# Attention, second half: ScalarE's operations on rows fetched from DRAM kept in program order, the last output weights split one tile later each

## The chip, the cores and the metric

The kernel runs on one core of a Trainium2 chip. The metric is the time of one execution on the device, in microseconds (us). Five engines work side by side, each through its own queue and in the order of that queue: TensorE (PE, matrix products), VectorE (DVE), ScalarE (ACT), GpSimd (POOL) and SyncE (SP), which here issues nearly all DMA transfers.

## The reference

One encoder layer on x of 2048 tokens by 1024 columns, in float32. The tokens form a grid of 32 rows by 64 columns.

```
h    = layernorm(x) * (1 + scale) + shift            # shift, scale, gate from silu(c) @ ada_w + ada_b
proj = h @ w_in                                      # 1024 x 9216
q_h, i_h, zf, zb, g_h, q_n, k_n, v_n, g_n = split(proj)
y_hg = rmsnorm(scan_forward + scan_backward) * silu(g_h)     # 8 heads of 128, gated linear recurrence
o_na = softmax(q k^T / 8 + bias, over an 8 x 16 window) v    # 16 heads of 64, on the grid
y_na = o_na * silu(g_n)
out  = layernorm(2**0.25 * x + gate * (concat(y_hg, y_na) @ w_out)) * ln_g + ln_b
```

The change touches the neighbourhood attention (q_n, k_n, v_n, g_n) of the second half of the tokens, and the preparation of w_out.

## The kernel before

Every large product is done in three passes on pairs of reduced-precision parts: a float32 operand is split into a high part (ScalarE copies it, which rounds) and a low part (VectorE subtracts the high part from the raw one). TensorE multiplies high by high, high by low and low by high. So a block of weights costs a DMA, one ScalarE operation and one VectorE operation before TensorE can use it.

The program has four stages: the attention of the first half of the tokens; the recurrence (`hgrn`) of both halves; the attention of the second half; and the rest of the output projection with the last layer norm. The change lies in the third, which is some 600 us long.

There the work goes in eight **units** u = 0 to 7, one for each pair of heads. A unit has twelve **tiles**: three groups of query rows R = 1, 2, 3 by four column blocks j. For a tile, `scores` multiplies Q by the keys (L1000, L1003), VectorE adds the bias and takes the maximum (L1012), ScalarE takes the exponential (L1017), VectorE normalises (L1021, L1022), TensorE transposes (`turned`, L1044), VectorE and ScalarE copy the transposes out of PSUM (L1048, L1050), and `sums` multiplies by V (L1063). After tile 4 of a row group the result is multiplied by the gate (L1073) and stored. A tile is turned one step, and summed two steps, after its scores.

While a unit's tiles run, TensorE fills the gaps with the dense products of the next unit (`natten_stream`, L278: q, k and gate columns), or in unit 7 with the first four token blocks of the output projection (`out_stream`, L1428 to L1430). `weave` deals these out by a running share, two steps per tile. In unit 0 the stream begins with the last products for v (`vstream`, L291, copied out of PSUM at L297).

After each tile i, `natten_woven` calls what its lists name for **slot** i: `prep_now` (this unit's last pieces), `prep_next` (the next unit's pieces) and `extra`. The pieces are those of `Prep`: `q(R)` makes two split Q tiles (L926 to L929), `k(i)` writes a piece of the shared key tiles KA, KB, KL (L941, then a DMA that copies the piece within the tile, L942, and L943), `gate(R)` takes silu (an exponential at L956, then `sigmoid`, L337 to L339, with two more ScalarE operations, and L958), `v(c)` loads V (L950), and `table` loads the bias (L722 to L730). Row groups 2 and 3 take q, k and gate from products that this stage has just made. Row group 1 and the first two key pieces belong to tokens of the first half: their products were stored in DRAM long ago, and `fetch` brings them back into four buffers `bk` (L913). There are four such buffers for four rows per unit (q, k0, k1, g), so a fetch waits until an earlier row has been used.

In units 6 and 7, `extra` also holds the preparation of the output weights: `wo_load(n, blocks)` loads blocks of 128 rows by 512 columns (column half n) into six buffers (four of `vt`, two of `gt`, L1383), and `wo_split` splits them (L1388, L1389) into tiles that held the dense products' left operand (`hts`). `y_early` and `y_split` do the same for the left operand of the output projection (L1394, L1420, L1421).

**What sets the order.** TensorE's queue in this stage is written out by hand: it is the program order. The other queues are ordered by a planner, which runs a simulated timeline over the program and issues, on each engine, the operation that it takes to be ready, the earlier in program order first; a block under `high_priority` counts as 1500 places earlier. It can move an operation far ahead of its place if the simulated transfer has landed by then. `keep_in_program_order` (called `pinned` in the file, L127) takes one operation and puts it behind the operation that was traced last before it on the same engine. It adds no wait. It holds against that one neighbour only: if the neighbour can move, the pinned operation can move with it. Before the change, `wo_split`, `y_split` and the split of the dense weights (L778) are pinned; `q`, `k` and `gate` are not.

Of the kernel before, what the change touches and what calls it, by code (L numbers as in the profile page):

```python
# [13 lines left out]
AF = mybir.ActivationFunctionType  # L14
# [24 lines left out]
def body(ctx: ExitStack, tc: tile.TileContext, t):  # L39
    nc = tc.nc  # L40
    dve, act, pool, pe = nc.vector, nc.scalar, nc.gpsimd, nc.tensor
    dma = nc.sync.dma_start
    x, out = t["x"], t["out"]
# [9 lines left out]
    @contextmanager  # L53
    def psum_phase(name, psb, pmap={}):
        with tc.tile_pool(name="p" + name, bufs=1, space=PSUM, reuse_waits="tile") as q:
            cur.update(psum=q, ps=psb, map=pmap)
            yield

    @contextmanager
    def phase(name, bufs, smap={}):  # L60
        with tc.tile_pool(name=name, bufs=1, reuse_waits="tile") as p:
            cur.update(pool=p, bufs=bufs, smap=smap)
            yield
# [28 lines left out]
    def tl(tag, dt=F32, shape=None):  # L92
        if tag in cur["smap"]:
            tag = cur["smap"][tag]
            return sh.tile([P, 512], dt, tag=tag, name=nm(tag), bufs=SH[tag])
        return cur["pool"].tile([P, 512] if shape is None else shape, dt, tag=tag, name=nm(tag), bufs=cur["bufs"].get(tag, 1))
# [50 lines left out]
    def mod_load(k):  # L147
        mod["w", k] = tl("ada", shape=[P, 2 * D])
        dma(mod["w", k], t["ada_m"][k])
# [186 lines left out]
    def sigmoid(e):  # L336
        dve.tensor_scalar_min(e, e, ECAP)  # L337
        act.activation(e, e, AF.Ln, bias=1.0)
        act.activation(e, e, AF.Exp, scale=-1.0)  # L339
# [331 lines left out]
    def bias_fill():  # L671
        bigt = tl("big", shape=[P, 448])
        pool.memset(bigt, BIG)
        rows = tint.rearrange("a j q r h k -> (a j q) (r h k)").rearrange("(x y) m -> y x m", y=P)
        src = bigt.rearrange("p (o m) -> p o m", o=1).to_broadcast([P, 3, 448])
        pinned(dma(rows[:, :, 0:448], src))
        pinned(dma(rows[:, :, 960:1408], src))
# [57 lines left out]
    def natten_init(n, half):  # L735
        pbuf.clear()
        cur["bias"] = (11, 15)[half]
        for i in range(n):
            b = tl("pbuf")
            pool.memset(b[:, 352:512], 0.0)  # L740
            pbuf.append(b)
        keysets.clear()
        for i in range(2 - half):
            keysets.append({z: tl(f"{z}{i}", F32R, [P, (12, 28)[half] * GW]) for z in ("KA", "KB", "KL")})
# [116 lines left out]
    def natten_stream(p, half, feed=None, bygroup=False):  # L861

        raws = {n: [None, None] for n, _ in NCOL}

        def gen():
            for gs in ((0,), (1,)) if bygroup else ((0, 1),):
                for n, c in NCOL:
                    if feed:
                        i = feed.at
                        feed.at += 1  # L870
                        feed.split(i + 1)
                        feed.load(i + 2)
                        his, los = feed.tiles[i]
                    else:
                        wv = t["w_in"][(c + p * P) // P]
                        his, los = load_split(lambda i: wv[:, i * 512:(i + 1) * 512], 2)
                    for g in gs:
                        pz = ps("pj")
                        for k in range(KT):
                            proj_mm(pz, his, los, g, k)  # L880
                            if k == KT - 1:
                                raws[n][g] = evac(pz)
                            if feed and g == gs[-1] and k == 2:
                                feed.split(i + 2)
                            yield KUS
        return raws, gen()
# [4 lines left out]
    def vstream(*pairs):  # L891
        for p2 in pairs:
            for _ in vproj(t["w_v"][p2], nv_d[p2], 1):
                yield 2.9
# [8 lines left out]
    class Prep:  # L903
# [17 lines left out]
        def q(self, R):  # L921
            raw = self.src("q", R)
            rv = raw.rearrange("p (r j c) -> p j r c", j=4, c=16)[:, :, ::-1, :]
            a, b = tl("Q", F32R), tl("Q", F32R)
            av, bv = (z.rearrange("p (j r c) -> p j r c", j=4, c=16) for z in (a, b))
            act.activation(av[0:64], rv[0:64], AF.Copy)  # L926
            act.activation(bv[64:128], rv[64:128], AF.Copy)
            dve.tensor_tensor(av[64:128], rv[0:64], av[0:64], op=ALU.subtract)
            dve.tensor_tensor(bv[0:64], rv[64:128], bv[64:128], op=ALU.subtract)  # L929
            self.Q[R] = (a, b)  # L930

        def k(self, i):
            a, b, src, off = KPIECE[self.half][i]
            n = (b - a) * GW
            raw = (self.bk[src] if src in self.bk else self.raws["k"][src])[:, off:off + n]
            o = slice(a * GW, b * GW)
            top, bot = slice(0, 64), slice(64, 128)
            keys = keysets[self.p % len(keysets)]
            for z, x, y in (("KA", top, bot), ("KB", bot, top)):
                z = keys[z]  # L940
                act.activation(z[x, o], raw[x], AF.Copy)  # L941
                dma(z[y, o].bitcast(F32), z[x, o].bitcast(F32))  # L942
                dve.tensor_tensor(keys["KL"][x, o], raw[x], z[x, o], op=ALU.subtract)  # L943

# [8 lines left out]
        def gate(self, R):  # L953
            raw = self.src("g", R)
            sg = tl("sg")
            act.activation(sg, raw, AF.Exp, scale=-1.0)  # L956
            sigmoid(sg)
            dve.tensor_tensor(sg, raw, sg, op=ALU.mult)  # L958
            self.sg[R] = sg
# [156 lines left out]
    def turn(pipe, n):  # L1116
        if len(pipe) >= n:
            m, r, c, ss = pipe[-n]
            pipe[-n][3] = m.turned(r, ss)
# [295 lines left out]
    def y_split(*tts):  # L1415
        for tt in tts:
            for q in range(2):
                hi = wp.tile([P, 512], F32R, tag="whi", name=nm("yh"), bufs=4)
                lo = wp.tile([P, 512], F32R, tag="wlo", name=nm("yl"), bufs=4)
                tc.keep_in_program_order(act.activation(hi, yraws[tt, q], AF.Copy))  # L1420
                dve.tensor_tensor(lo, yraws[tt, q], hi, op=ALU.subtract)  # L1421
                yhl[tt, q] = hi, lo
# [70 lines left out]
    with psum_phase("n1", NPS), phase("n1", NB1, SM1), tc.manual_schedule(engines={mybir.EngineType.PE}):  # L1493
        natten_init(5, 1)
        st = st0
        for f, *a in ((st.k, 0), (st.k, 1), (st.k, 2), (st.q, 1), (st.table, "mid", 0), (st.table, "mid", 1), (st.v, 2), (st.v, 3), (st.table, "mid", 3), (st.q, 2), (st.v, 4), (st.gate, 1)):
            f(*a)
        vs = vstream(2, 3)
        for _ in range(5):
            next(vs)  # L1500
        pipe = []
        cts = [(c + u * P) // P for u in range(1, 8) for _ in range(2 if u == 7 else 1) for n, c in NCOL]
        feed = Feed(cts)
        feed.at = 0
        for u in range(8):
            nxt, extra = None, None
            if u < 7:
                raws, dense = natten_stream(u + 1, 1, feed, u + 1 == 7)
                total = NLEN
                if u == 0:  # L1510
                    dense, total = chain(vs, dense), NLEN + 1.375 * VLEN
                nxt = Prep(u + 1, 1, raws)
                if u == 6:
                    extra = {4: [(wo_load, 0, 0, 1)], 5: [(wo_load, 0, 2, 3, 4, 5)], 7: [(wo_split, 0, 0, 1)], 8: [(wo_split, 0, 2, 3), (wo_load, 0, 6, 7)],
                             9: [(wo_split, 0, 4, 5)], 10: [(wo_split, 0, 6, 7), (wo_load, 1, 0, 1, 4, 5), (y_early, 0)], 11: [(wo_load, 1, 2, 3), (y_early, 1)]}
            else:
                y_split(0, 1)
                dense, total = out_stream(list(range(NE))), NE * 16 * KUS
                extra = {0: [(wo_split, 1, 0, 1), (wo_load, 1, 6, 7)], 1: [(wo_split, 1, 2, 3)], 2: [(wo_split, 1, 4, 5, 6, 7)]}
            weave(natten_woven(st, nxt, pipe, extra), dense, total, 24)  # L1520
            st = nxt
        m, r, c, pts = pipe.pop(0)
        m.sums(r, c, pts)
        turn(pipe, 1)
        m, r, c, pts = pipe.pop(0)
        m.sums(r, c, pts)
# [72 lines left out]
```

## Time and profile before

| | us |
|---|---|
| three runs: median (lowest, highest) | 2688.76 (2688.58, 2693.19) |
| the profiled execution | 2689.12 |
| span of its profile | 2687.3 |
| TensorE busy in the span | 2607.6 (97%) |
| VectorE, ScalarE busy | 1766.4 (66%), 1421.6 (53%) |
| second half of the attention | about 1764 to 2374 |

The time of an execution holds the span of the profile and a little around it. In the rows below an instruction has its start, its duration, its engine, its line in the kernel, the tile that it writes and those that it reads, and in brackets how long its engine had been idle before it and what ended that. A busy share alone does not tell what a microsecond saved on an engine is worth; that is read from where TensorE waits, and for whom.

### The profile page before, as it was taken

The page shows a single profiled execution, that of the slowest core. Times are in us where ns is not written, and L with a number is a line of the kernel's source. Part 1 is how long each engine was busy: PE and PEld are TensorE (multiplying, and loading weights), DVE is VectorE, ACT ScalarE, POOL GpSimd, SP SyncE. Part 2 cuts the span into 40 slices and gives each one's busy share as a digit, 9 for nine tenths or more (in the row PEclk, how much of TensorE's full clock was granted, in tenths as well). Part 3 has the DMA queues.
Part 4 walks back from the last instruction along what each step waited for, and adds up shares of the span by engine and source line. Part 5 has one row for each costly group of instructions (what it writes and reads, how often), then busy time and mean ns, then how long its engine had stood idle before and what let it go on. Part 6 is the DMA issues. An engine that isn't in the chain of part 4 may idle for free.

```text
span 2687.3 us, 46049 instructions
## 1 busy us (share of the span) xinstructions
PE 2607.6 (97%) x17332; PEld 2153.6 (80%) x17332; DVE 1766.4 (66%) x4354; ACT 1421.6 (53%) x2808; POOL 105.8 (4%) x142
## 2 busy tenths in 40 slices
PE   6999999989999999999999999989999999899998
PEld 5888788878888888888888888877777777678887
DVE  7445545377777778778877787445777778548443
ACT  4533445366666666666666666445666666431110
POOL 0000000000000000000000000000000000032221
PEclk8999999999999999999999999999999999999999
DMA  7476454212111136212222222344444445344331
GB/s 270 138 210 146 139 174 143 87 49 72 64 60 60 64 94 212 72 44 71 75 71 79 66 71 91 106 141 127 128 127 128 128 131 142 101 146 133 98 94 55
DMA packets 225550, 295.94 MB, mean 110 GB/s; under 512 B 28599, under 2 KB 117431, under 8 KB 224183
## 3 DMA queue, kind: packets, MB, share of 16 engines
q1 hardware_dynamic: 225327, 293.00, 36.0%
q8 instruction: 136, 2.23, 0.4%
q14 instruction: 87, 0.71, 0.1%
HBM read 217.72 MB, written 66.99 MB: 106 GB/s over the span
## 4 chain that ended last, share of the span: by engine, by line
PE 72%; DVE 2%; DMA 2%; ACT 1%; issue 1%; SPq 0%; DVEq 0%; ACTq 0%
PE pj L278 39%; PE ps L1428 4%; PE ps L1430 4%; PE ps L1429 4%; PE ps L1063 3%; PE ps L1044 3%; PE pj L291 2%; PE ps L478 2%; PE ps L1000 1%; PE ps L470 1%; PE ps L1003 1%; PE ps L545 1%; PE ps L569 1%; PE ps L517 1%; PE ps L571 1%; PE ps L643 1%
## 5 line engine op out<-in xcount | busy, mean ns | idle before, releaser
L278 PE MATMUL pj<-h,wh 128*128 128x512 f32 x4000 | 1277.0, 400 | 4.5 <-ACT wh L803 2.1
L278 PEld LDWEIGHTS pj<-h,wh 128*128 128x128 f32 x4000 | 722.6, 188 | 162.5 <-issue 21.4
L278 PE MATMUL pj<-h,wl 128*128 128x512 f32 x2000 | 783.5, 392 | 0.0
L278 PEld LDWEIGHTS pj<-h,wl 128*128 128x128 f32 x2000 | 375.4, 188 | 83.1 <-DVE wl L804 0.4
L1017 ACT ACTIVATE pbuf<-pbuf,mx 128x480 f32<-128x480 f32 (+2 forms) x256 | 164.3, 643 | 182.3 <-DVE mx L1012 181.5
L1012 DVE CUSTOM_DVE_ANT_1 pbuf<-ps,bias 128x480 f32<-128x480 f32 (+2 forms) x256 | 144.1, 595 | 134.6 <-PE ps L1003 121.4
L291 PE MATMUL pj<-wh,h 128*128 128x256 f32 x1024 | 199.3, 289 | 10.2 <-ACT vt L297 9.9
L291 PEld LDWEIGHTS pj<-wh,h 128*128 128x128 f32 x1024 | 165.6, 194 | 14.9 <-ACT vt L297 10.8
L268 ACT ACTIVATE wh<-wr 128x512 fp32r<-128x512 f32 x192 | 120.2, 626 | 79.6 <-PE pj L278 69.1
L269 DVE TENSOR_TENSOR wl<-wr,wh 128x512 fp32r<-128x512 f32 x192 | 131.5, 685 | 42.9 <-ACT wh L268 41.4
L291 PE MATMUL pj<-wl,h 128*128 128x256 f32 x512 | 146.0, 285 | 0.0
L1050 ACT ACTIVATE pt<-ps 128x512 f32<-128x512 f32 (+1 forms) x128 | 69.0, 539 | 124.2 <-PE ps L1044 124.0
L1044 PE MATMUL ps<-ident,pbuf 128*128 128x128 f32 x896 | 119.4, 273 | 11.1 <-DVE pbuf L1022 11.1
L1048 DVE COPY pt<-ps 128x512 f32<-128x512 f32 (+1 forms) x128 | 79.3, 620 | 75.7 <-PE ps L1044 74.8
L1044 PEld LDWEIGHTS ps<-ident,pbuf 128*128 128x128 f32 x896 | 105.4, 141 | 27.2 <-issue 12.3
L464 DVE TENSOR_TENSOR de<-e,de 128x512 f32<-128x512 f32 x64 | 44.3, 692 | 118.7 <-ACT de L463 118.7
L1022 DVE TENSOR_SCALAR pbuf<-pbuf,mx 128x480 f32<-128x480 f32 (+2 forms) x256 | 107.9, 438 | 5.0
L1063 PE MATMUL ps<-pt,V 128*64 128x128 f32 x1376 | 104.3, 282 | 4.1 <-DVE pt L1048 3.4
L1404 ACT ACTIVATE yh<-yr 128x512 fp32r<-128x512 f32 x52 | 32.6, 628 | 129.3 <-PE ps L1429 107.2
L291 PEld LDWEIGHTS pj<-wl,h 128*128 128x128 f32 x512 | 99.3, 194 | 1.4 <-issue 0.5
L1477 DVE TENSOR_TENSOR vt<-ps,gt 128x512 f32<-128x512 f32 x24 | 16.5, 692 | 127.0 <-PE ps L1430 127.0
L1063 PEld LDWEIGHTS ps<-pt,V 128*64 128x64 f32 x1376 | 73.3, 136 | 31.1 <-issue 18.4
(268 smaller groups left out, 4646.9 us busy)
## 6 DMA issues: line engine op xcount, KB each, us to landing
wr<-in_w_in SPq DMA_DIRECT2D x276, 256.0 KB
yr<-yq SPq DMA_DIRECT2D x64, 256.0 KB
V<-nv SPq DMA_DIRECT2D x248, 64.0 KB
bias<-tint SPq DMA_DIRECT2D x24, 480.0 KB
x<-in_x SPq DMA_DIRECT2D x32, 256.0 KB
ada<-in_ada_m SPq DMA_DIRECT2D x8, 1024.0 KB
wr<-in_w_v SPq DMA_DIRECT2D x32, 256.0 KB
nv<-vt SPq DMA_DIRECT2D x32, 256.0 KB
```

Of the source, the lines that this page charges most:

```text
L268: act.activation(hi, raw, AF.Copy)
L269: dve.tensor_tensor(lo, raw, hi, op=ALU.subtract)
L278: pe.matmul(pz, a, b, start=(k == 0 and n == 0), stop=(k == KT - 1 and n == 2))
L291: pe.matmul(pzs[tp][:, i * 256:(i + 1) * 256], a, b, start=(k == 0 and n == 0 and i == 0), stop=(k == KT - 1 and n == 2), skip_group_check ...
L1012: return dve.tensor_tensor_reduce(s[:, 0:nk].rearrange("p (r c) -> p r c", c=32), sc[:, 0:nk].rearrange("p (r c) -> p r c", c=32), bt[:, 0 ...
L1017: act.activation(s[:, 0:nk], s[:, 0:nk], AF.Exp, scale=-1.0, bias=mx[:, 0:1], accum_out=mx[:, 1:2])
L1022: dve.tensor_scalar(s[:, 0:nk], s[:, 0:nk], mx[:, 2:3], 1.0, op0=ALU.mult, op1=ALU.mult)
L1044: pe.transpose(ptp[:, c * P:(c + 1) * P], s[:, c * P:(c + 1) * P], ident)
L1063: pe.matmul(self.po[R][hs_, j * P:(j + 1) * P], self.st.V[c0 + c][:, j * P + hh * 64:j * P + hh * 64 + 64], pts[hh][:, c * P:(c + 1) * P], ...
L1428: pe.matmul(pz, yh[:, kk], wh, start=first, stop=False)
L1429: pe.matmul(pz, yh[:, kk], wl, start=False, stop=False)
L1430: pe.matmul(pz, yl[:, kk], wh, start=False, stop=last)
```

## The change

There are two edits. The first pins ScalarE's operations of `q`, `k` and `gate` where their source is a row fetched from DRAM (row group 1, key pieces k0 and k1); where the source is a product of this stage, nothing changes. The second moves splits and loads of output weights to later slots: blocks (6, 7) of column half 0 are split in slot 0 of unit 7 and no longer in slot 10 of unit 6; of column half 1, blocks 0 and 1 in slot 1 (before: 0), blocks 2 and 3 in slot 2 (before: 1), blocks 4 and 5 in slot 2 as before, blocks 6 and 7 in slot 3 (before: 2). The loads of blocks 2 and 3 of column half 1 move from slot 11 of unit 6 to slot 0 of unit 7, and those of blocks 6 and 7 from slot 0 to slot 1. No operation is added or removed.

```diff
@@ Prep.q
-            act.activation(av[0:64], rv[0:64], AF.Copy)
-            act.activation(bv[64:128], rv[64:128], AF.Copy)
+            keep = pinned if raw is self.bk.get("q") else lambda x: x
+            keep(act.activation(av[0:64], rv[0:64], AF.Copy))
+            keep(act.activation(bv[64:128], rv[64:128], AF.Copy))
@@ Prep.k
+            keep = pinned if src in self.bk else lambda x: x
             for z, x, y in (("KA", top, bot), ("KB", bot, top)):
                 z = keys[z]
-                act.activation(z[x, o], raw[x], AF.Copy)
+                keep(act.activation(z[x, o], raw[x], AF.Copy))
@@ Prep.gate
-            act.activation(sg, raw, AF.Exp, scale=-1.0)
+            keep = pinned if raw is self.bk.get("g") else lambda x: x
+            keep(act.activation(sg, raw, AF.Exp, scale=-1.0))
@@ unit 6 (tiles 4 to 11) and unit 7
                     extra = {4: [(wo_load, 0, 0, 1)], 5: [(wo_load, 0, 2, 3, 4, 5)], 7: [(wo_split, 0, 0, 1)], 8: [(wo_split, 0, 2, 3), (wo_load, 0, 6, 7)],
-                             9: [(wo_split, 0, 4, 5)], 10: [(wo_split, 0, 6, 7), (wo_load, 1, 0, 1, 4, 5), (y_early, 0)], 11: [(wo_load, 1, 2, 3), (y_early, 1)]}
+                             9: [(wo_split, 0, 4, 5)], 10: [(wo_load, 1, 0, 1, 4, 5), (y_early, 0)], 11: [(y_early, 1)]}
...
-                extra = {0: [(wo_split, 1, 0, 1), (wo_load, 1, 6, 7)], 1: [(wo_split, 1, 2, 3)], 2: [(wo_split, 1, 4, 5, 6, 7)]}
+                extra = {0: [(wo_split, 0, 6, 7), (wo_load, 1, 2, 3)], 1: [(wo_split, 1, 0, 1), (wo_load, 1, 6, 7)], 2: [(wo_split, 1, 2, 3, 4, 5)], 3: [(wo_split, 1, 6, 7)]}
```

## The prediction

> **What bounds the kernel now.** I read the profile's page first, then the busy time in stretches of 50 us, then what TensorE (PE) waited for, then ScalarE (ACT), VectorE (DVE), SyncE (SPq) and PE instruction by instruction around the two holes that the stretches show. First the page's part 1, then three of the stretches (columns: PE, PE weight loads, DVE, ACT, POOL busy, granted clock, DMA share, GB/s), then the two longest rows of PE's waits (total, times, longest).
>
> ```profile
> PE 2607.6 (97%) x17332; PEld 2153.6 (80%) x17332; DVE 1766.4 (66%) x4354; ACT 1421.6 (53%) x2808; POOL 105.8 (4%) x142
> ```
>
> ```profile
> 1750.00:1800.00 50.00, 38.22 (x287) 34.97 (x287) 22.62 (x51) 20.73 (x41) 0.00 (x0) 0.90 0.52 147
> ...
> 1900.00:1950.00 50.00, 49.48 (x341) 38.20 (x340) 37.83 (x115) 31.52 (x73) 0.61 (x2) 1.00 0.47 125
> ...
> 2250.00:2300.00 50.00, 37.70 (x240) 28.33 (x237) 36.04 (x98) 29.53 (x67) 0.31 (x1) 0.90 0.71 166
> ```
>
> ```profile
> PE ps L1044 <- DVE pbuf L1022: 11.1, 2, 10.9
> PE pj L291 <- ACT vt L297: 9.9, 2, 9.0
> ```
>
> PE is the bound, busy 97% of the span, and in most of the second half (1900 to 1950 is typical) there is next to nothing to win. But two stretches lack some 12 us of PE each, and have a granted clock of 0.90. So a change that touches neither stretch is worth nothing, and one that fills both is worth over 20 us. Both holes lie in what this change edits.
>
> **Hole A, at 1776 to 1786**, one unit after the second half begins (ACT, SPq, then PE):
>
> ```profile
> 1784.55 0.63 ACT L956 ACTIVATE sg<-bk 128x512 f32<-128x512 f32 x1 [9.26 <-DMA bk<-ng]
> 1785.09 0.58 ACT L297 ACTIVATE vt<-pj 128x512 f32<-128x512 f32 x1
> ```
>
> ```profile
> 1781.10 0.32 SPq L913 DMA_DIRECT2D bk<-ng  x1
> ```
>
> ```profile
> 1785.72 0.58 PE L291 MATMUL pj<-wh,h 128*128 128x256 f32 x1 [8.96 <-ACT vt L297]
> ```
>
> The exponential of the gate of unit 1, row 1, stands in ACT's queue before the copy of a full PSUM bank (L297). It waits 9.26 us for its row, which SyncE only issued at 1781.10; the copy behind it waits along, and PE waits 8.96 us for the bank. The gate is written in slot 11 of unit 0: the planner has put it some ten tiles ahead of its place.
>
> **Hole B, at 2282 to 2293**, first tile of unit 7 (SPq; ACT; DVE; PE):
>
> ```profile
> 2277.94 3.65 SPq L1383 DMA_DIRECT2D vt<-in_w_out  x1
> ```
>
> ```profile
> 2274.59 1.15 ACT L1388 ACTIVATE wo<-vt 128x512 fp32r<-128x512 f32 x2
> ...
> 2289.38 0.63 ACT L1388 ACTIVATE wo<-vt 128x512 fp32r<-128x512 f32 x1 [10.76 <-DMA vt<-in_w_out]
> ```
>
> ```profile
> 2281.03 0.22 DVE L1021 RECIPROCAL mx<-mx 128x1 f32<-128x1 f32 x2
> 2290.05 0.69 DVE L1389 TENSOR_TENSOR wo<-vt,wo 128x512 fp32r<-128x512 f32 x1 [8.79 <-ACT wo L1388]
> ...
> 2292.21 0.41 DVE L1022 TENSOR_SCALAR pbuf<-pbuf,mx 128x384 f32<-128x384 f32 x1
> ```
>
> ```profile
> 2281.44 0.40 PE L1430 MATMUL pj<-wo,yl 128*128 128x512 f32 x1
> 2292.77 1.53 PE L1044 MATMUL ps<-ident,pbuf 128*128 128x128 f32 x6 [10.94 <-DVE pbuf L1022]
> ```
>
> Counting the L1388 rows through in the order of the calls, the one that waits is block (2, column half 1), the first of `wo_split(1, 2, 3)` in slot 1 of unit 7. It is pinned, but only behind the ScalarE operation traced just before it, the last of gate(2), which is itself free to move; so it could still come ahead of the first tile's exponentials. Its load was issued at 2277.94, because its buffer is one that (6, 0) held. DVE's low part of it stands in front of the softmax shares (L1022) of the tile before, and PE waits for those to transpose.
>
> **Edit 1: gate, q and k on fetched rows are pinned.** Nothing is added or removed; per unit two operations of q(1), two each of k(0) and k(1), one of the gate change place. Gate(1) of the next unit is now pinned in slot 11 behind the last copy out of PSUM that was traced, which depends on PE and cannot float. That takes it out of hole A. Gain: the 8.96 idle, and the slow clock after it, from the windows of 5 us:
>
> ```profile
> 1785.00:1790.00 5.00, 4.28 (x19) 4.28 (x20) 1.81 (x3) 2.82 (x6) 0.00 (x0) 0.50 0.60 206
> 1790.00:1795.00 5.00, 5.00 (x43) 3.98 (x43) 2.51 (x8) 1.47 (x4) 0.00 (x0) 0.91 0.39 115
> ...
> 2290.00:2295.00 5.00, 2.23 (x9) 1.90 (x10) 4.53 (x12) 4.97 (x12) 0.00 (x0) 0.50 0.98 217
> 2295.00:2300.00 5.00, 5.00 (x29) 3.67 (x28) 2.43 (x9) 1.14 (x4) 0.00 (x0) 0.89 0.23 63
> ```
>
> Lost to the clock after A: 4.28 x 0.50 + 5.00 x 0.09 = 2.6; after B: 2.23 x 0.50 + 5.00 x 0.11 = 1.7. A is worth 8.96 + 2.6 = 11.6. The Trainium skill (TensorE: Matmul & The Clock Gate, "Part 1: The HAM clock gate") has the clock fall to half after an idle window of about 3.4 us and come back after about as much steady work. By that alone a hole would cost half of 3.4 us beside its idle time, 3.4 for both in place of 4.3, and the sum below would end 0.9 higher; the trace agrees that both holes are followed by a clock of 0.50.
>
> Where the gate goes, unit 2 as an example (ACT; DVE; PE):
>
> ```profile
> 2007.48 0.58 ACT L752 ACTIVATE e<-pj 128x512 f32<-128x512 f32 x1
> ...
> 2009.08 0.70 ACT L1017 ACTIVATE pbuf<-pbuf,mx 128x480 f32<-128x480 f32 x1 [0.36 <-DVE mx L1012]
> ...
> 2015.76 0.63 ACT L956 ACTIVATE sg<-bk 128x512 f32<-128x512 f32 x1
> ```
>
> ```profile
> 2016.71 0.42 DVE L337 TENSOR_SCALAR sg<-sg 128x512 f32<-128x512 f32 x1
> ...
> 2018.76 0.69 DVE L958 TENSOR_TENSOR sg<-bk,sg 128x512 f32<-128x512 f32 x1 [1.03 <-ACT sg L339]
> ```
>
> ```profile
> 2008.28 0.44 PE L1063 MATMUL ps<-pt,V 128*64 128x128 f32 x4 [0.51 <-DVE pt L1048]
> ...
> 2015.88 1.04 PE L1044 MATMUL ps<-ident,pbuf 128*128 128x128 f32 x8
> ```
>
> It leaves 2015.76 for the seam after 2007.48. Its three ACT operations (0.63 each) and two of DVE (0.42, 0.69) are 3.0 us. Behind them stand the exponentials at 2009.08, whose shares PE needs only at 2015.88; those 6.8 us cover 3.0. So I take 0 per seam. The ends are a gain of 0.51 (the wait at 2008.28 goes with the new order) and a loss of 3.0 (all of it before something that PE needs at once); seven seams.
>
> Unit 0's own gate(1), and what hangs on its buffer (ACT, SPq, PE):
>
> ```profile
> 1657.28 0.62 ACT L956 ACTIVATE sg<-bk 128x512 f32<-128x512 f32 x1
> ```
>
> ```profile
> 1663.06 0.32 SPq L913 DMA_DIRECT2D bk<-nq  x1
> ```
>
> ```profile
> 1764.19 0.46 PE L1000 MATMUL ps<-KA,Q 128*128 128x480 f32 x1 [1.88 <-DMA V<-nv]
> ```
>
> It ran at 1657, and is now pinned to the start of the second half, about 1755. Its 3.0 us lie ahead of a copy out of PSUM there, but PE waits 1.88 for a transfer at 1764.19 anyway: cost 0, at most 3.0 - 1.88 = 1.1. Its row buffer is freed 100 us later too, so the fetch issued at 1663.06 joins SyncE's queue after 1755, one transfer more there. The pinned Q of unit 1 needs it some 30 us later: 0.
>
> k(1) moves by about two tiles, k(0) likewise; their DMA copies within KA and KB move with them past the loads of V (the rival on the slow side, below). In the likeliest case they land before the next unit's first scores: 0.
>
> **Edit 2: the splits one or two tiles later.** (6,0) and (7,0) go from slot 10 to slot 0, to about where (0,1), (1,1) ran at 2274.59, long landed. (0,1), (1,1) go to the loose slot 1, in the place of the pair that stalled, their data also there. (2,1) to (5,1) are now in slot 2, where four splits ran already:
>
> ```profile
> 2310.41 1.14 ACT L1388 ACTIVATE wo<-gt 128x512 fp32r<-128x512 f32 x2
> ```
>
> That slot follows a copy from PE, so it cannot float; in the new time it stands about 10 us earlier, near 2300, and the load that landed at 2289.38 is in time by 10 us. The two loads moved to unit 7's slot 0 wait for the buffers of (6,0), (7,0), as before, now free after about 2278; SyncE issued there at 2277.94 anyway. What is left of hole B: the DVE operations ahead of the shares (2290.05 to 2292.21, 2.16 us) would still stand there. From 2281.25 that gives 2283.4 for the shares, 0.56 more to PE's transposes (2292.21 to 2292.77), 2283.97 against PE's end at 2281.84: 2.1 us of waiting stay. At best 0 stay; at worst the gate's 3.0 come on top in this seam, 5.1. I take 2.1, since the same places in the order are filled again. B is worth 10.94 + 1.7 - 2.1 = 10.5.
>
> **Sum.** The profiled execution took 2689.12 (span 2687.3 and 1.8 around it), 0.4 above the median of 2688.76, which is nothing here. 2689.12 - 11.6 - 10.5 = 2667.0.
>
> **Rivals.** (a) A wait that takes B's place. PE arrives 10 us earlier at work fed by the busiest DMA stretch (0.98 in 2290 to 2295): the tables of bias of unit 7's second tile or blocks (6,1), (7,1). For it: the load of 2277.94 took 11.4 us. Against it: (2,1) and (3,1) now have 10 us to spare. If one lands 6 us late: 6 + 1.7 for the clock, 2667 + 7.7 = 2674.7. (b) The change does half of what it says: a pin holds only behind its neighbour, and hole B shows a pinned operation floating. Then A or B stays, 2678.6 or 2677.5. Against it for A: slot 11's neighbour is tied to PE. (c) No change: the gate's 3.0 us count in full at all seven seams, 21.0, 2688. Against it: the 6.8 us of cover. (d) Slower, by the copies of k(1) (ACT; SPq; PE):
>
> ```profile
> 1980.80 0.42 ACT L941 ACTIVATE KA<-bk 64x256 fp32r<-64x256 f32 x1 [0.95 <-DMA bias<-tedge]
> ...
> 1990.58 0.60 ACT L1050 ACTIVATE pt<-ps 128x512 f32<-128x512 f32 x1 [1.55 <-PE ps L1044]
> ```
>
> ```profile
> 1993.03 1.91 SPq L950 DMA_DIRECT2D V<-nv  x3
> ...
> 1995.50 3.90 SPq L950 DMA_DIRECT2D V<-nv  x5
> ```
>
> ```profile
> 1758.44 5.69 SPq L950 DMA_DIRECT2D V<-nv  x4
> ```
>
> ```profile
> 2006.75 0.38 PE L1000 MATMUL ps<-KA,Q 128*128 128x480 f32 x1
> ```
>
> Pinned in slot 8, k(1) leaves 1980.80 for about 1991, behind the copy of 1990.58. If its copies queue behind the eight loads of V, they go out at 1999.4, the four take 2.6 to issue (1.91 / 3 each) and, like bk<-ng (1781.10 to 1784.5), 3.4 to land: 2005.4, before 2006.75 by 1.3. If each V load takes 1.42 to issue, as the four at 1758.44 did, the eight end at 2004.4, the copies land at 2010.4, PE waits 3.6 and loses about 1.7 to the clock: 5.3 in each of seven units, 37, so 2704. It decides from a wait of 3.2 per unit (22.1 / 7). Against it: SyncE issues one in 0.64 to 0.78 there, and copies ready at 1991 can go ahead of the loads.
>
> **Numbers.** Forecast (2660 to 2672) 0.61; (a) 0.17; (b) 0.08; (c) 0.08; (d) 0.06. Low end: the 2.1 and seven waits of 0.51 go too, 2661, and a little more for a new order elsewhere: 2660. High end past (a) and (b): 2682. That leaves out (c) and (d) and a fringe of the rest, 2 in 10. A measurement of this kernel tells 0.2% from nothing, 5.4 us: faster is the forecast, (a) and (b), 0.86; same (c), 0.08; slower (d), 0.06.
>
> **What would show it.** Right: no L956 on bk waiting for a DMA; the 1750 to 1800 stretch has PE near 48 us and clock 1.00; the splits of (2,1) come after tile 1 of unit 7 and wait for nothing; L1044 waits for L1022 about 2 us near its start. Wrong: PE waits for KA, KB at first tiles of units (d), PE waiting for L1022, L1048 or L752 at seams (c), a new wait of ACT for a DMA near 2290 to 2300 (a). The forecast fails most simply if the planner, given other constraints from 1657 on, lays out the queues of the whole second half anew and puts some other operation ahead of its data.

## The result and the profile after

| | before | after |
|---|---|---|
| median of five runs (lowest to highest), us | 2691.09 (2688.58 to 2693.19) | 2673.56 (2672.58 to 2676.06) |
| the profiled execution; span of its profile, us | 2689.12; 2687.3 | 2676.06; 2674.3 |

The ratio is 0.9938, with a 95% interval of 0.9928 to 0.9949: the change makes the kernel faster by 0.6%, 17.5 us by the medians. The forecast was 22.1 us (2667.0). The time lies inside the forecast range (2660 to 2682), but above the part of it that the forecast itself was given (2660 to 2672), and 4 to 5 us of the gain are missing.

Some lines of the kernel have moved by two or three: L956 is now L959, L1022 is L1025, L1044 is L1047, L1388 is L1391, L1394 is L1397, L1420 is L1423, L1428 is L1431; L291 and L297 stand where they stood. First the page's part 1 and the three stretches of 50 us of the changed kernel (columns as before), then the longest of what PE waited for between 1640 and 2380 (total, times, longest).

```profile
PE 2608.6 (98%) x17332; PEld 2154.6 (81%) x17332; DVE 1765.3 (66%) x4354; ACT 1420.1 (53%) x2808; POOL 105.5 (4%) x142
```

```profile
1750.00:1800.00 50.00, 46.96 (x386) 43.63 (x384) 30.07 (x66) 29.33 (x59) 0.00 (x0) 1.00 0.59 168
1900.00:1950.00 50.00, 49.48 (x338) 38.13 (x337) 39.40 (x114) 34.98 (x80) 0.61 (x2) 1.00 0.53 136
2250.00:2300.00 50.00, 44.41 (x281) 33.85 (x276) 37.00 (x106) 32.89 (x73) 0.00 (x0) 0.93 0.63 164
```

```profile
PE pj L1431 <- ACT yh L1423: 6.3, 2, 5.1
PE ps L1066 <- DVE pt L1051: 3.9, 8, 0.6
PE pj L291 <- ACT vt L297: 2.5, 1, 2.5
PE ps L350 <- DVE rh L345: 2.1, 2, 1.4
PE pj L278 <- ACT wh L778: 1.3, 1, 1.3
```

The wait of 9.0 us for the copy L297 and that of 10.9 for the shares (L1022, now L1025) are both gone. The 2.5 us for L297 that the list still has are another wait, at 1763.76 (0.94 us in the kernel before): the gates of unit 0 now stand ahead of that copy. They cost next to nothing, since the wait of 1.88 for V that followed has shrunk to 0.55 (row of 1767.43 below). The first stretch is nearly whole again: PE 46.96 in place of 38.22, at a clock of 1.00. The third is not: 44.41 in place of 37.70, with a clock of 0.93. A new wait stands there, at the seam (the passage from one unit to the next) of units 6 and 7: 5.1 us of L1431, the first product of the output projection, for `yh`, the high part of its left operand. ScalarE and PE of the changed kernel around it, and its windows of 5 us:

```profile
2271.42 0.62 ACT L959 ACTIVATE sg<-bk 128x512 f32<-128x512 f32 x1
2271.94 1.14 ACT L959 ACTIVATE sg<-e 128x512 f32<-128x512 f32 x2
...
2274.33 1.66 ACT L338 ACTIVATE sg<-sg 128x512 f32<-128x512 f32 x3
2275.89 0.62 ACT L339 ACTIVATE sg<-sg 128x512 f32<-128x512 f32 x1
2276.41 2.18 ACT L1423 ACTIVATE yh<-yr 128x512 fp32r<-128x512 f32 x4
```

```profile
2271.25 0.70 PE L1066 MATMUL ps<-pt,q 128*64 128x128 f32 x7
2277.08 0.79 PE L1431 MATMUL pj<-wo,yh 128*128 128x512 f32 x1 [5.13 <-ACT yh L1423]
```

```profile
2275.00:2280.00 5.00, 2.92 (x7) 2.22 (x8) 4.45 (x11) 5.00 (x10) 0.00 (x0) 0.50 0.88 219
2280.00:2285.00 5.00, 5.00 (x25) 3.67 (x23) 2.52 (x5) 1.16 (x3) 0.00 (x0) 0.84 0.98 237
```

No row of ScalarE has a bracket there: it waits for nothing, it works through a queue. The copies to `yh` are pinned, and what `y_split` was traced behind is gate(1) of unit 7, which the change has pinned to slot 11 of unit 6. So they start at 2276.41, right behind that gate's last operation (L339 at 2275.89), while PE is free from 2271.95. The clock is lost along with it: 2.92 x 0.50 + 5.00 x 0.16 = 2.3 us by the windows. Matmul by matmul 1.6 of it is found: from the start of this product to that of the ninth (2277.08 to 2280.66) pass 3.58 us, and with the second edit alone (below, 2280.45 to 2282.40) 1.95.

**Where the time went, matmul by matmul.** PE's order is the same in all kernels here, so the start of one matmul can be subtracted between two traces. Three such pairs, before and after: 1764.19 and 1767.43 (first scores of unit 0), 2006.75 and 2000.05 (the first of unit 2), 2297.11 and 2284.03 (the second tile of unit 7); the first two of before stand in the prediction. The third of before, then the three of after:

```profile
2297.11 0.39 PE L1000 MATMUL ps<-KA,Q 128*128 128x480 f32 x1
```

```profile
1767.43 0.46 PE L1003 MATMUL ps<-KA,Q 128*128 128x480 f32 x1 [0.55 <-DMA V<-nv]
...
2000.05 0.38 PE L1003 MATMUL ps<-KA,Q 128*128 128x480 f32 x1
...
2284.03 0.38 PE L1003 MATMUL ps<-KA,Q 128*128 128x480 f32 x1
```

The differences are +3.2, -6.7 and -13.1. The table does this for every kernel of the study: how much the difference to the trace of before grows in each stretch, in us (minus is time saved; the stretches are by the clock of the kernel before; medians over the matmuls within 3 us of each border).

| kernel | to 1640 | 1640 to 1675 | 1675 to 1772 | A: 1772 to 1800 | 1800 to 2200 | B: 2200 to 2300 | behind | sum |
|---|---|---|---|---|---|---|---|---|
| the change | +1.79 | +1.55 | -0.09 | -11.48 | +1.53 | -6.37 | +0.02 | -13.05 |
| first edit alone | +1.66 | +1.58 | +0.24 | -11.49 | +0.05 | -5.82 | 0.00 | -13.78 |
| second edit alone | +0.58 | -0.02 | +0.60 | +0.20 | +0.04 | -12.38 | 0.00 | -10.98 |
| change, y_split free | +1.81 | +0.07 | +0.81 | -11.48 | +0.01 | -4.14 | +0.01 | -12.91 |
| change, gate of unit 7 free | +2.37 | +1.54 | -0.67 | -11.49 | 0.00 | -3.39 | -0.01 | -11.65 |
| change, gate pinned alone | +0.25 | +0.03 | +0.70 | -11.49 | +0.03 | -5.19 | -0.01 | -15.68 |
| change, q and k pinned alone | +1.72 | -0.04 | +3.13 | -2.45 | 0.00 | -4.48 | -0.01 | -2.13 |
| one gate and the second edit | +1.47 | +1.56 | -0.12 | -11.48 | +0.66 | -12.35 | -0.01 | -20.27 |
| change, block 0 of y early | +1.27 | +1.49 | -0.73 | -11.49 | +0.01 | -11.81 | +0.01 | -21.25 |

The steps of some 1.5 us up to 1675 and behind 1800 are not put down to the change: PE's work and its waits there are the same, and the clock is not (last section). The changed kernel's profiled execution drew three of them, 4.6 us in all, that of before none. So between these two profiles 13 us are seen, between the medians 17.5, and the change itself is worth 11.48 in A and 6.37 in B, 17.9.

### The profile page after: what moved, and what is told of

Read it like the earlier page. It is cut to its first block, busy times and chain, and to the rows that moved or that the text cites. A ratio compares the mean times of both kernels' runs of the same rounds, so it can differ in the third digit from the quotient of the medians.

```text
span 2674.3 us, 46068 instructions
## 1 busy us (share of the span) xinstructions
PE 2608.6 (98%) x17332; PEld 2154.6 (81%) x17332; DVE 1765.3 (66%) x4354; ACT 1420.1 (53%) x2808; POOL 105.5 (4%) x142
## 4 chain that ended last, share of the span: by engine, by line
PE 73%; DVE 2%; DMA 1%; ACT 1%; issue 1%; SPq 0%; DVEq 0%; ACTq 0%
PE pj L278 39%; PE ps L1431 4%; PE ps L1433 4%; PE ps L1432 4%; PE ps L1066 3%; PE ps L1047 3%; PE pj L291 2%; PE ps L478 2%; PE ps L470 1%; PE ps L1003 1%; PE ps L1006 1%; PE ps L545 1%; PE ps L569 1%; PE ps L517 1%; PE ps L571 1%; PE ps L643 1%
## 5 line engine op out<-in xcount | busy, mean ns | idle before, releaser
L291 PE MATMUL pj<-wh,h 128*128 128x256 f32 x1024 | 196.7, 287 | 2.8 <-ACT vt L297 2.5
L291 PEld LDWEIGHTS pj<-wh,h 128*128 128x128 f32 x1024 | 163.5, 192 | 7.2 <-ACT vt L297 3.2
L291 PE MATMUL pj<-wl,h 128*128 128x256 f32 x512 | 144.9, 283 | 0.0
L1053 ACT ACTIVATE pt<-ps 128x512 f32<-128x512 f32 (+1 forms) x128 | 69.4, 542 | 135.3 <-PE ps L1047 134.7
L1051 DVE COPY pt<-ps 128x512 f32<-128x512 f32 (+1 forms) x128 | 79.3, 619 | 78.1 <-PE ps L1047 76.7
L1047 PE MATMUL ps<-ident,pbuf 128*128 128x128 f32 x896 | 118.9, 273 | 0.0
L1047 PEld LDWEIGHTS ps<-ident,pbuf 128*128 128x128 f32 x896 | 105.5, 141 | 15.6 <-issue 0.4
L1025 DVE TENSOR_SCALAR pbuf<-pbuf,mx 128x480 f32<-128x480 f32 (+2 forms) x256 | 107.6, 437 | 4.8
L291 PEld LDWEIGHTS pj<-wl,h 128*128 128x128 f32 x512 | 98.2, 192 | 1.4 <-issue 0.5
L752 ACT ACTIVATE e<-pj 128x512 f32<-128x512 f32 x98 | 58.4, 596 | 76.3 <-PE pj L278 70.8
```

The source lines that it names most:

```text
L291: pe.matmul(pzs[tp][:, i * 256:(i + 1) * 256], a, b, start=(k == 0 and n == 0 and i == 0), stop=(k == KT - 1 and n == 2), skip_group_check ...
L1025: dve.tensor_scalar(s[:, 0:nk], s[:, 0:nk], mx[:, 2:3], 1.0, op0=ALU.mult, op1=ALU.mult)
L1047: pe.transpose(ptp[:, c * P:(c + 1) * P], s[:, c * P:(c + 1) * P], ident)
```

## The experiments

Each kernel was timed beside the kernel before (its median was 2691.53 us beside the first four and 2690.9 beside the others).

### The first edit alone

The pins, with the slots and loads of before:

```diff
-                             9: [(wo_split, 0, 4, 5)], 10: [(wo_load, 1, 0, 1, 4, 5), (y_early, 0)], 11: [(y_early, 1)]}
+                             9: [(wo_split, 0, 4, 5)], 10: [(wo_split, 0, 6, 7), (wo_load, 1, 0, 1, 4, 5), (y_early, 0)], 11: [(wo_load, 1, 2, 3), (y_early, 1)]}
...
-                extra = {0: [(wo_split, 0, 6, 7), (wo_load, 1, 2, 3)], 1: [(wo_split, 1, 0, 1), (wo_load, 1, 6, 7)], 2: [(wo_split, 1, 2, 3, 4, 5)], 3: [(wo_split, 1, 6, 7)]}
+                extra = {0: [(wo_split, 1, 0, 1), (wo_load, 1, 6, 7)], 1: [(wo_split, 1, 2, 3)], 2: [(wo_split, 1, 4, 5, 6, 7)]}
```

> The first edit alone: the pins, with the slots of before. Account of the prediction (two separate gains): only hole A near 1776 goes, 11.5 us off the before kernel; hole B stays, because block (2, half 1) is still split in slot 1 of unit 7 and floats ahead of its data: PE waits some 10 us for L1022's successor near the start of unit 7. Rival (the pins reach further): gate(1) of unit 7 is now tied to its slot, y_split is pinned behind it and the splits of slots 0 and 1 behind y_split, so nothing in that chain can float; then hole B goes without the second edit, and the time is that of the changed kernel, some 17.5 us off, with a PE wait of about 5 us for yh (L1420 of before) in its place.

Measured: 2674.54 us, ratio 0.9941 (0.9929 to 0.9954), as the whole change. What PE waited for between 2262 and 2300, then rows of ScalarE and one of SyncE (by the line numbers of after):

```profile
PE pj L1431 <- ACT yh L1423: 5.1, 1, 5.1
```

```profile
2265.76 1.16 ACT L1391 ACTIVATE wo<-vt 128x512 fp32r<-128x512 f32 x2
...
2270.69 1.14 ACT L959 ACTIVATE sg<-e 128x512 f32<-128x512 f32 x2
...
2277.25 0.61 ACT L339 ACTIVATE sg<-sg 128x512 f32<-128x512 f32 x1
2277.77 1.14 ACT L1391 ACTIVATE wo<-vt 128x512 fp32r<-128x512 f32 x2
...
2296.65 1.14 ACT L1391 ACTIVATE wo<-gt 128x512 fp32r<-128x512 f32 x2
```

```profile
2265.94 0.89 SPq L1386 DMA_DIRECT2D vt<-in_w_out  x1
```

The rival holds in its outcome. Hole B goes without the second edit: blocks 2 and 3 of column half 1, of which the first stalled before, are split at 2277.77 and wait for nothing (their first load was issued at 2265.94). And the wait of 5.1 us takes B's place here too, so the second edit did not make it.

The chain that the rival names is right for the copies to `yh`, but not for the splits. The split of slot 0 (2265.76) runs ahead of all three gates of the unit, so it does not hang behind `y_split`. Blocks 2 and 3 hang where the prediction had them, behind the last operation of gate(2) (L339 at 2277.25). What is new is that gate(2), which nobody pinned, stays at the seam (2270.69, the first of the two) and no longer floats ahead (2243.24 in the kernel before). In all ten traces, and in each of the eight units, gate(1) runs ahead of the other two gates, and where it is pinned late they follow close behind it: with one gate pinned, that of unit 1 (further below), the three run in a row in that unit alone (1865.26, then 1865.78 x2). Why the planner keeps that order is not shown.

### The second edit alone

The slots and loads of after, none of the pins (against the changed kernel):

```diff
-            keep = pinned if raw is self.bk.get("q") else lambda x: x
-            keep(act.activation(av[0:64], rv[0:64], AF.Copy))
-            keep(act.activation(bv[64:128], rv[64:128], AF.Copy))
+            act.activation(av[0:64], rv[0:64], AF.Copy)
+            act.activation(bv[64:128], rv[64:128], AF.Copy)
...
-                keep(act.activation(z[x, o], raw[x], AF.Copy))
+                act.activation(z[x, o], raw[x], AF.Copy)
...
-            keep(act.activation(sg, raw, AF.Exp, scale=-1.0))
+            act.activation(sg, raw, AF.Exp, scale=-1.0)
```

> The second edit alone: the later slots, with no new pins. Account of the prediction: hole A stays (PE waits 9.0 for L297), hole B gives 10.5 us, of which 2.1 us of waiting stay in any case. Rival (the 5.1 us that PE waits for yh in the changed kernel come from the pinned gate of unit 7): without the pins the yh copies run at 2260 to 2277 as before, PE does not wait for yh, and B gives 12 to 13.5 us. Second rival (the wait comes from the later slots): B gives only about 6 us.

Measured: 2678.97 us, ratio 0.9956 (0.9944 to 0.9969). PE's longest wait between 1640 and 2380, then all its waits between 2270 and 2300 (by the line numbers of before):

```profile
PE pj L291 <- ACT vt L297: 10.5, 2, 9.6
```

```profile
PE ps L1063 <- DVE pt L1048: 0.4, 1, 0.4
PE ps L1044 <- DVE pbuf L1022: 0.2, 1, 0.2
```

A stays, as both expected. B gives 12.4 us, and of the 2.1 us that the prediction left there 0.2 is found. So the first rival holds: the 5.1 us belong to the pins. Each edit fills hole B by itself, and the edit that does it worse decides when both are in.

### One pin less: y_split free

```diff
-    def y_split(*tts):
+    def y_split(*tts, keep=pinned):
...
-                tc.keep_in_program_order(act.activation(hi, yraws[tt, q], AF.Copy))
+                keep(act.activation(hi, yraws[tt, q], AF.Copy))
...
-                y_split(0, 1)
+                y_split(0, 1, keep=lambda x: x)
```

> The changed kernel with one pin taken away: y_split(0, 1), the four copies to yh for the first output products, is no longer kept in program order. If PE's 5.1 us at the first output product (and the half clock behind it, some 2.3) are there because these four copies hang behind the pinned gate(1) of unit 7, the copies move up to where their rows have landed, the wait goes, and the kernel is 5 to 7.4 us faster than the changed one, 22 to 25 off the before kernel. If it is ScalarE's pile of work at the seam as such (three gates, Q, keys, splits), something else of that pile is late in their place and less than 2 us come back.

Measured: 2675.37 us, ratio 0.9944 (0.993 to 0.9957): not faster than the change. ScalarE, PE and SyncE of this kernel:

```profile
2273.88 0.63 ACT L1423 ACTIVATE yh<-yr 128x512 fp32r<-128x512 f32 x1 [6.63 <-DMA yr<-yq]
```

```profile
2276.13 0.47 PE L1066 MATMUL ps<-pt,V 128*64 128x128 f32 x1 [7.19 <-ACT pt L1053]
```

```profile
2253.84 3.52 SPq L952 DMA_DIRECT2D V<-nv  x4
...
2259.74 2.60 SPq L952 DMA_DIRECT2D V<-nv  x4
...
2264.07 0.57 SPq L1397 DMA_DIRECT2D yr<-yq  x1
...
2265.37 3.82 SPq L1397 DMA_DIRECT2D yr<-yq  x3
```

The wait for `yh` did go, as expected, and another took its place. That nothing comes back is what the second account had, but for a cause that neither had. The planner put the third copy (token block 1) ahead of the exponentials and of the copy of the transposes (L1053), but its row was only issued behind eight loads of V. This is how holes A and B of the kernel before were made. Whether ScalarE's pile of work would have been next is not decided by this run. It does show that the splits do not hang on `y_split`: with the copies free, the split of slot 1 still runs at 2283.22, right behind gate(2)'s last operation at 2282.70.

### Gate(1) of unit 7 alone free

```diff
-            keep = pinned if raw is self.bk.get("g") else lambda x: x
+            keep = pinned if raw is self.bk.get("g") and self.p < 7 else lambda x: x
```

> The changed kernel with gate(1) of unit 7 alone not pinned. It then runs some ten tiles early, as before the change. Both accounts of the 5.1 us (the pin chain, the pile of ScalarE work at the seam) expect the wait to go here: 5 to 7.4 us faster than the changed kernel. It risks the kind of wait that made hole A: if its row is not there, ScalarE waits for a DMA; in the kernel before it had landed in this unit, so 0 for that. If the first products still wait 5 us, both accounts fall.

Measured: 2676.28 us, ratio 0.9945 (0.9933 to 0.9958). The gate moved early, the wait for `yh` went, and ScalarE waits for the row of the third copy instead:

```profile
2276.59 0.63 ACT L1423 ACTIVATE yh<-yr 128x512 fp32r<-128x512 f32 x1 [6.75 <-DMA yr<-yq]
```

Both accounts expected the time back and missed, for the reason of the run above. With the second edit alone the gate and the copies are just as free, and PE waits 0.4 us at most at this seam. So something else in the first edit makes the rows of y late. That leaves the pins of q and k and those of the other units' gates; the next two runs part them.

### The gate pinned alone, and q and k pinned alone

```diff
-            keep = pinned if raw is self.bk.get("q") else lambda x: x
+            keep = lambda x: x
...
-            keep = pinned if src in self.bk else lambda x: x
+            keep = lambda x: x
```

> The changed kernel with only the gate pinned; q and k on fetched rows are free again. If the gate's pin alone fills hole A, nothing is lost there: 11.5 us off the before kernel up to 1800. At the seam of unit 7 the copies to yh still hang behind gate(1), so PE still waits some 5 us for yh, and the time is that of the changed kernel, 17 us off. Rival: the pins of q and k, which shift the order of the transfers, are what makes the rows of y late there; then the wait for yh shrinks below 2 us and the kernel is 4 to 6 us faster than the changed one.

```diff
-            keep = pinned if raw is self.bk.get("g") else lambda x: x
+            keep = lambda x: x
```

> The changed kernel with only q and k pinned; the gate is free. Hole A stays (PE waits 9 us for L297 near 1780). At the seam of unit 7 the gate is early and the copies to yh are free to float. If the pins of q and k delay the rows of y (the transfers of V then go ahead of them), a copy to yh again comes ahead of its row and PE waits 7 us for the copy of the transposes behind it, as in the kernel with unit 7's gate free: about 5 to 6 us off the before kernel in all. If they do not, PE waits for nothing there, as with the later slots alone: 12 us off.

Measured: the gate alone 2674.6 us, ratio 0.9944 (0.993 to 0.9957); q and k alone 2685.87 us, ratio 0.9978 (0.9969 to 0.9988). ScalarE's copies with the gate pinned alone, then ScalarE and SyncE with q and k pinned alone:

```profile
2272.57 0.61 ACT L339 ACTIVATE sg<-sg 128x512 f32<-128x512 f32 x1
2273.09 2.17 ACT L1423 ACTIVATE yh<-yr 128x512 fp32r<-128x512 f32 x4
```

```profile
2286.27 0.63 ACT L1423 ACTIVATE yh<-yr 128x512 fp32r<-128x512 f32 x1 [6.73 <-DMA yr<-yq]
```

```profile
2264.73 3.23 SPq L952 DMA_DIRECT2D V<-nv  x4
2270.35 2.60 SPq L952 DMA_DIRECT2D V<-nv  x4
2275.15 1.25 SPq L1397 DMA_DIRECT2D yr<-yq  x2
```

The gate's pin alone does all of A (-11.49) and alone makes the wait for `yh`: all four copies again stand right behind L339, and PE waits 5.1. The pins of q and k do nothing for A as a whole (3.13 lost just ahead of it, 2.45 won in it; PE still waits 6.6 us for L297), give 5 us in all by the medians, as the first case of that expectation has it, and put the loads of V ahead of the rows of y (by which of the planner's choices is not shown). With the second edit alone the order of these two is the other way round:

```profile
2262.74 1.83 SPq L1394 DMA_DIRECT2D yr<-yq  x2
2264.66 6.30 SPq L950 DMA_DIRECT2D V<-nv  x3
```

So the first edit holds two separate costs at this seam: the gate's pin drags the copies of y back, and q's and k's pins make it unsafe to let them go.

### One gate and the second edit

```diff
-            keep = pinned if raw is self.bk.get("q") else lambda x: x
+            keep = lambda x: x
...
-            keep = pinned if src in self.bk else lambda x: x
+            keep = lambda x: x
...
-            keep = pinned if raw is self.bk.get("g") else lambda x: x
+            keep = pinned if raw is self.bk.get("g") and self.p == 1 else lambda x: x
```

> The later slots, and one single pin: gate(1) of unit 1, the operation that made hole A. q, k and the other gates are free. If the holes are independent and nothing else in the change is worth anything, A gives 11.5 and B the 12 that the later slots alone gave: 23.5 us off the before kernel, 6 faster than the changed one, no PE wait over 1.5 us between 1770 and 2370. Rival: a new order of the transfers in every unit moves another operation ahead of its data, and part of it is lost to a wait elsewhere: not faster than the changed kernel.

Measured: 2669.34 us, ratio 0.9924 (0.9912 to 0.9937). By the medians this is 21.6 us off the kernel before; in A and B together it is 23.8, as expected. No PE wait over 1.3 us is left between 1770 and 2370. Beside the later slots, one was needed of the eight pinned gates and of all the pins of q and k.

### All pins kept, block 0 of y early

```diff
-(wo_load, 1, 0, 1, 4, 5), (y_early, 0)], 11: [(y_early, 1)]}
+(wo_load, 1, 0, 1, 4, 5), (y_early, 0), (y_split, 0)], 11: [(y_early, 1)]}
...
-                y_split(0, 1)
+                y_split(1)
```

> The changed kernel, all pins kept, with the copies to yh of token block 0 split in slot 10 of unit 6, ahead of gate(1) of unit 7; those of block 1 stay pinned behind it. The rows of block 0 landed by 2250, those of block 1 only near 2274. If the wait of 5.1 us is the first output product waiting for a copy pinned too late, it goes and with it the half clock, 5 to 7.4 us faster than the changed kernel. If the seam is bound by ScalarE's and VectorE's pile of work, the next operation in the pile is late (the shares for L1047, the copy L1053) and less than 2 us come back.

Measured: 2668.86 us, ratio 0.9921 (0.9908 to 0.9935). ScalarE's copies of y, and PE's longest waits between 1770 and 2370:

```profile
2261.21 1.14 ACT L1423 ACTIVATE yh<-yr 128x512 fp32r<-128x512 f32 x2
...
2273.67 1.15 ACT L1423 ACTIVATE yh<-yr 128x512 fp32r<-128x512 f32 x2
```

```profile
PE ps L1066 <- DVE pt L1051: 4.0, 8, 0.6
PE pj L278 <- ACT wh L778: 1.3, 1, 1.3
PE pj L1431 <- ACT yh L1423: 1.2, 1, 1.2
```

The pile of gates on ScalarE is still there, and only two copies left it for a place twelve microseconds earlier; the wait of 5.1 is gone, and B gives 11.81 in place of 6.37, 5.4 more. So most of what the seam cost came from the place of one copy and not from the amount of work on ScalarE. The pile is not quite free: matmul by matmul the gain over the change is 7.0 us behind the first products and 5.4 at the end of the seam, and 0.9 of that loss are two new waits of 0.5, for DVE's reciprocal (L1024) and for the copy L1053. This version and the one above have the lowest medians of the study, 4.2 and 4.7 us below the change, and the slowest time of each is below the fastest of the change (2672.58). The intervals of the ratios overlap with that of the change (0.9928 to 0.9949); that the gain is some 5 to 6 us rests on the matmuls set side by side.

## Why the prediction was right, and where it was not

The time lies in the stated range, but partly by luck. The sum was 6.6 us short of it, and the part of the range that the forecast itself was given ended at 2672. What carries the range past 2673.56 are rivals (a) and (b), and the cause of neither was found. (The kernel before also came out 2.3 us slower in the final count, 2691.09, than in the three runs that the sum started near.) The mechanism was right for hole A and wrong in one term of hole B.

- **Hole A** (11.6 forecast): 11.48 or 11.49 in each kernel that pins the gate of unit 1, and 11.48 where that is the only pin. Idle time plus half clock was the right price, and the instruction named was the cause.
- **Seams, at 0 each; rival (c)**: between 1800 and 2200 the table shows at most 0.05 in all for the kernels with all gates pinned, once the changed kernel's step of clock is set aside. PE's waits for L1051 come to 3.9 us in the whole stretch, against 3.4 for L1048 before. The cover of 6.8 us held, and held more than it was priced for: at each seam all three gates now run in a row (for example at 2202.59, then 2203.11 x2), where the prediction moved one.
- **Unit 0's gate, at 0 to 1.1**: from 1675 to 1772 the kernels with all the gate pins lie between -0.73 and +0.81, and the change itself at -0.09. Here too gates 2 and 3 came along (1762.07 x2; before, at 1709.7 and 1726.6).
- **k(1); rival (d)**: wrong in a step of its own. The copies in `KA` and `KB` were issued ahead of the loads of V and not behind them, and PE's first scores waited for nothing (SyncE; the row of PE at 2000.05 above has no bracket):

```profile
1984.81 0.52 SPq L944 DMA_DIRECT2D KA<-KA  x1
1985.43 0.55 SPq L944 DMA_DIRECT2D KB<-KB  x1
1986.33 1.75 SPq L952 DMA_DIRECT2D V<-nv  x3
```

- **Hole B** (10.5 forecast, 6.37 measured): the step that failed is "I take 2.1, since the same places in the order are filled again". It priced the seam as if the second edit stood alone, and watched the shares for PE's transposes. Its own sign, that L1044 waits some 2 us for L1022, is missing: PE waits 0.2 there with the second edit alone, and nothing with both edits. What became late, by 5.1 us, is the operand of the product that PE issues ahead of them, because the first edit gave `y_split` a fixed neighbour. The end of 5.1 that the prediction gave for this seam came about in size by another way: it was three gate operations ahead of the shares; found was a pinned chain ahead of `yh`, with 1.6 to 2.3 of half clock on top, which that end had not counted. That the two sizes agree is chance.
- **Rival (a)** named the place and, by luck, nearly the price (2674.7): a wait in B's place. Its cause, a late transfer of bias or of blocks (6,1), (7,1), was not found; no operation of ScalarE waits for a DMA at this seam in the changed kernel. It was found only when the copies were set free, with the rows of y.
- **Rival (b)**, that A or B stays because a pin holds only behind its neighbour, fell: both went. What the prediction took from it also fell, that the loose split needs the second edit: with the pins alone B goes. "Behind its neighbour" was read one step deep. The split of slot 1 hangs behind gate(2), and gate(2), though not pinned, does not pass gate(1): once gate(1) is fixed, the split is. The copies of `y_split` hang behind gate(1) directly. With gate(1) of unit 7 free, gate(2) was early again (2237.04). Why it never passes gate(1) stays open.
- **The last sentence**, a planner that lays out the queues anew, came true in the transfers of V and y, and cost nothing as long as the copies of y were held.
- **The sum**: 2689.12 - 11.48 - 6.37 = 2671.3, and 4.6 us of clock that the profiled execution lost elsewhere give 2675.9, against 2676.06. The median of five, 2673.56, lies between these two sums.

## What to carry to other kernels

A pin ties more than the operation it is put on: a pinned one that is traced right behind it hangs on it, and here two gates without a pin came along as well. Before adding one, follow the chain to its end, look in the new trace for what else moved, and ask which of these operations another engine needs first. Two edits that fill the same hole do not add up: run each alone, since here one pin and the later slots were worth 6 us more than the whole change. And where a scheduler may hoist an operation ahead of its data, moving it in the program to where the data has landed brought 5.4 us here, while letting it go only made another one stall as long as q and k were pinned.

## What the runs showed of the hardware

The same short wait of PE is followed by half clock in one execution and by none in another. PE waits 2.12 us at about 280 in both profiles; the rows are PE and the window that follows, of before, then of after:

```profile
280.33 0.73 PE L278 MATMUL pj<-h,wh 128*128 128x512 f32 x2 [2.12 <-ACT wh L803]
```

```profile
282.00:284.00 2.00, 2.00 (x17) 1.45 (x17) 0.56 (x2) 0.00 (x0) 0.00 (x0) 1.00 0.86 270
```

```profile
280.19 0.73 PE L278 MATMUL pj<-h,wh 128*128 128x512 f32 x2 [2.12 <-ACT wh L803]
```

```profile
282.00:284.00 2.00, 2.00 (x7) 1.62 (x5) 0.06 (x1) 0.00 (x0) 0.00 (x0) 0.50 0.91 274
```

It costs 1.5 us each time. Of the ten profiles here six have it at 280, five at 1663 (behind waits of 1.38 and 0.23) and one, the changed kernel's, at 1815 (behind a wait of 1.26). Three of them make a difference of up to 4.6 us between two executions of the same work, a quarter of what this change is worth; the five times of the kernel before lie as far apart. That is the size of the gap between the two profiles, 13 us apart, and the medians, 17.5 apart; the executions that were not profiled cannot be read for such drops. The Trainium skill (TensorE: Matmul & The Clock Gate, "Part 1: The HAM clock gate") has a free-running window of about 3.4 us, so that the moment of the switch varies from run to run; the traces here agree in so far as the drop comes in some executions and not in others, and the window itself they do not show. The same page of the Trainium skill ("Why this matters for your kernels") warns of idle gaps above some 3 us; the traces differ, since here the clock fell once behind a wait of 1.26 us and in six of ten behind one of 2.12, so a shorter wait is not safe.
